# Squares without a ring slot, a weight ring in reverse, and retention products with two heads in turn, in a transformer layer on one core

## The chip, the cores and the metric

The kernel runs on one core of a Trainium2 chip. The core has five engines with instruction streams of their own: TensorE (PE; its weight loads are shown as PEld), VectorE (DVE), ScalarE (ACT), GpSimd (POOL) and SyncE (SP), which issues most of the DMAs. They meet only in semaphores. The metric is the device time of one execution in microseconds; of several timed runs the median counts.

## The reference

One layer over 1024 tokens of width 1024, in float32: a norm, one input projection, a gated causal convolution, an eight-head retention, a mix of the two, a mixture of 32 experts (two for each token) and a gated addition of a second input p.

```python
h = rmsnorm(x, g_mix)
u, c_g, b_g, q, k, v, sg, m_c, m_r = split(h @ w_in)
y_conv = (b_g * causal_dwconv(c_g * u, conv_w)) @ w_out_conv
q, k = rope(q), rope(k) * RET_DK ** -0.5          # 8 heads of 64
o = retention(q, k, v)                             # v: 8 heads of 128
y_ret = (silu(sg) * rmsnorm(o, g_ret)) @ w_out_ret
x = x + (sigmoid(m_c) * y_conv + sigmoid(m_r) * y_ret) @ w_o
x = x + hier_moe(rmsnorm(x, g_moe), ...)
ple = rmsnorm(p @ w_ple_proj, g_ple_post)
x = x + sigmoid(rmsnorm(x, g_ple_in) @ w_ple_gate) * ple
return rmsnorm(x, g_final)

def retention(q, k, v):      # chunks of 128 tokens; state: 64 x 128 for each head
    for each chunk:
        scores = (qb @ kb.T) * decay_mask
        inner  = scores @ vb
        cross  = (qb @ state) * q_decay
        state  = state * chunk_decay + (kb * k_decay).T @ vb
        out    = inner + cross
```

## The kernel before

The program runs in stages, whose times in the profiled execution are: the norm of x, its transpose and the projection to q, k, v, in two halves of 512 tokens (0 to 208 us); the gate sg with one retention chunk in each of eight steps (208 to 441); the convolution and the other gates (441 to 744); the mix and its projection (744 to 1020); the router and the projection of p (1020 to 1062); 32 experts (1062 to 1640); the last gate and norm (from 1646).

**Products.** Most matmuls work on a split: `split` (lines 186 to 190) has ScalarE write the high part of a tile (L188) and VectorE the rest (L189), and `mm3` (L193, L194, L195) multiplies high by high, high by low and low by high. The third needs the low part of its left operand. The retention's own products (scores L335, outputs L349 and L353, kv L369) are plain float32, and the trace shows each of them as two instructions.

**Order.** The program is written as one sequence; a scheduler sets the order on each engine by its own estimates, within what `tc.issue_after` binds. An engine then works through its order strictly, so an instruction that waits holds all behind it. Tiles come from pools: a pool's tag has a number of slots, and the first write to a tile waits until the tile that last held the slot has been read, by a DMA too. The tag `w2k` has ten slots of 2 KB a partition (`NW = 10`) and serves most scratch tiles.

**Squares.** `sumsq` (L218 to L222) takes the sum of squares of a block of 128 tokens on ScalarE; its elementwise output, which nothing reads, goes to a `w2k` slot (`xssj`). In `norm_T` (L224) each of the four blocks of a half is squared, scaled on VectorE by its rstd (`xrs`, `xi`, L235), transposed on TensorE (`xtq`, `xtp`, L240) and split into `ha` and `hb`, from which the projection `qa` reads. In `ple` (L781) the square `pj` (L805) of each half block takes a slot too, and so does the product `po` (L806, L807), which a DMA writes to the buffer `pled` in DRAM (L808): sixteen such transfers in all.

**Retention.** `retention(n, ck)` gives four steps that are put between the seven products of a gate pair: `turned` (transposes of q and k), `scores`, `outputs`, `close`. Tile `qt[r, a_]` holds in rows 0 to 63 head 2·a_ and in rows 64 to 127 head 2·a_+1, so a product of one head uses half the rows of TensorE. `scores` does the four even heads into bank `tr`, then the four odd ones into bank `S`. `outputs` fills one bank with heads 0 to 3 and one with heads 4 to 7: scores times v, and the state product of two heads at once, whose state tile is zero where the heads do not belong together. The next chunk's `turn` transposes the result and writes it to `od`.

**Experts.** The weights come as halves h = 0, 1, 2, ... of 1 MB into `raw` tiles (L746). `prep` (L921) splits each into one of three buffers `hls[h % RING]`: high part on ScalarE (L928), low part on VectorE (L930). `expert_x` (L942) transposes the gathered tokens (`xp`, L949) and splits them (`xh`, `xl`). These pools are opened where those of the stages before end, so `xl` and the buffers of the ring wait, at their first write, for the last use of what lay at their addresses.

Of the kernel before, what the change touches and what calls it, by code (L numbers as in the profile page):

```python
# [12 lines left out]
BF = mybir.dt.bfloat16  # L13
I32 = mybir.dt.int32
AF = mybir.ActivationFunctionType
OP = mybir.AluOpType
# [14 lines left out]
NW = 10  # L31
# [44 lines left out]
def tile_kernel(ctx, tc, cst, x, p, g_mix, w_in, conv_w, g_ret, w_out_conv, w_out_ret, w_o, g_moe,  # L76
# [140 lines left out]

    def sumsq(src, name, pool=wk):  # L218
        s = pool.tile([128, 8], F32, name=name, tag="sm", bufs=4)
        j = pool.tile([128, 1024], BF, name=name + "j", tag="w2k", bufs=NW)  # L220
        A.activation(j, src, AF.Square, accum_out=s[:, 0:1])
        return s[:, 0:1]  # L222

    def norm_T(hf, xi, gx):  # L224
# [67 lines left out]
    def bank(name, tag):  # L292
        return ps.tile([128, 4, 128], F32, name=name, tag=tag, bufs=1)

    def turn(n):
        t0 = n * 128
        for b in range(2):
            pt = bank("otp", ("o", "kv")[b])
            for j in range(4):
                pe = T.transpose(pt[:, j], osb[b][:, j], ident).ins  # L300
            ot = w2k("ot").rearrange("p (a b) -> p a b", a=4)
            for j in range(4):
                A.activation(ot[:, j], pt[:, j], AF.Copy, scale=gret[:, 4 * b + j:4 * b + j + 1])
            Y.dma_start(out=od[b * 512:(b + 1) * 512, t0:t0 + 128].rearrange("(a p) t -> p a t", p=128), in_=ot)
        return pe


    def retention(n, ck):
        first, last = n == 0, n == 7
        Y.dma_start(out=ck, in_=qd[n * 128:(n + 1) * 128])  # L310
        q, k, v = ck[:, 0:512], ck[:, 512:1024], ck[:, 1024:2048]
        qt, kt = (w2k(n_).rearrange("p (a b) -> p a b", a=4) for n_ in ("qt", "kt"))
        sm, rss, kvs = [], [], []

        def turned(pe):
            for src, dst_, tag in ((q, qt, "tr"), (k, kt, "S")):
                pt = bank("qkp", tag)
                for a_ in range(4):
                    pe = T.transpose(pt[:, a_], src[:, a_ * 128:(a_ + 1) * 128], ident).ins
                if src is q:  # L320
                    V.tensor_tensor(dst_, pt, qdT, op=OP.mult)
                else:
                    A.activation(dst_, pt, AF.Copy)
            if not first:
                with tc.issue_after(pe):
                    pe = turn(n - 1)
            return pe

        def scores(pe):
            for par in range(2):  # L330
                sp = bank("sp", ("tr", "S")[par])
                r = slice(par * 64, par * 64 + 64)
                with tc.issue_after(pe):
                    for a_ in range(4):
                        pe = T.matmul(sp[:, a_], kt[r, a_], qt[r, a_], start=True, stop=True).ins  # L335
                sb = w2k("sb").rearrange("p (a b) -> p a b", a=4)
                V.tensor_tensor(sb, sp, caus[:, None, :].to_broadcast([128, 4, 128]), op=OP.mult)
                sm.append(sb)
            return pe

        def outputs(pe):
            for b in range(2):
                op = bank("op", ("o", "tr")[b])
                m_ = 0
                with tc.issue_after(pe):
                    for a_ in (2 * b, 2 * b + 1):
                        for par in range(2):
                            h = 2 * a_ + par
                            pe = T.matmul(op[:, h - 4 * b], sm[par][:, a_], v[:, h * 128:(h + 1) * 128],  # L349
                                          start=m_ == 0, stop=first, skip_group_check=True).ins  # L350
                            m_ += 1
                        if not first:
                            pe = T.matmul(op[:, (a_ % 2) * 2:(a_ % 2) * 2 + 2], qt[:, a_],  # L353
                                          state[:, a_].rearrange("p (u v) -> p u v", u=2), start=False, stop=True,
                                          skip_group_check=True).ins
                A.activation(osb[b], op, AF.Copy)
                sq = w2k("osq").rearrange("p (a b) -> p a b", a=4)
                A.activation(sq, op, AF.Square)
                ss = wk.tile([128, 8], F32, name="oss", tag="sm", bufs=4)
                V.tensor_reduce(ss[:, 0:4], sq, axis=AX.X, op=OP.add)  # L360
                rss.append(rstd(ss[:, 0:4], DV, "ors"))
            if last:
                return pe
            kvs.append(bank("kv", "kv"))
            with tc.issue_after(pe):
                for a_ in range(4):
                    for par in range(2):
                        h = 2 * a_ + par
                        pe = T.matmul(kvs[0][par * 64:par * 64 + 64, a_], k[:, h * 64:h * 64 + 64],  # L369
                                      v[:, h * 128:(h + 1) * 128], start=True, stop=True, skip_group_check=True).ins  # L370
            return pe

        def close():
            for b in range(2):
                V.tensor_tensor(osb[b], osb[b], rss[b][:, :, None].to_broadcast([128, 4, 128]), op=OP.mult)
            for par in range(0 if last else 2):
                r = slice(par * 64, par * 64 + 64)
                sv = state[r, :, par * 128:par * 128 + 128]
                V.tensor_tensor(sv, sv, kvs[0][r], op=OP.add)
                V.tensor_tensor(sv, sv, Gd[r, :, None].to_broadcast([64, 4, 128]), op=OP.mult)  # L380

        return [turned, scores, outputs, close]


# [397 lines left out]
    def ple(wpl, pin):  # L782
# [12 lines left out]
        for t in range(8):  # L795
            pp = pps[t]
            for b in range(2):
                cc = slice(b * 512, (b + 1) * 512)
                a = acc("pa")
                for k in range(2):  # L800
                    r0 = k * 1024 + b * 512
                    mm3(a, pp[:, 0, k], pp[:, 1, k], wpl[:, r0:r0 + 512], wpl[:, 2048 + r0:2560 + r0],
                        k == 0, k == 1)
                j = w2k("pj", BF)[:, 0:512]
                A.activation(j, a, AF.Square, accum_out=ss[:, t, b:b + 1])  # L805
                o = w2k("po")  # L806
                V.tensor_tensor(o, a, gp[b], op=OP.mult)  # L807
                Y.dma_start(out=pled[t * 128:(t + 1) * 128, cc], in_=o)  # L808
                if b == 0 and t < 6:
                    pps.append(turned(t + 2))  # L810
# [103 lines left out]


    hls = [t.rearrange("p (s n) -> p s n", s=2) for t in (first_hl, mt("ha"), mt("hb"))]
    hls[1:] = hls[:0:-1]
    done = [0]

    def prep(n):  # L920
# [346 lines left out]
```

## Time and profile before

| | |
|---|---|
| timed runs, us | 1774.49, 1774.91, 1778.44; median 1774.91 |
| profiled execution, us | 1771.04, of which span 1769.2 |
| TensorE busy, us | 1708.2 (97%), 8063 matmul instructions |
| VectorE, ScalarE, GpSimd busy, us | 1265.4, 903.2, 157.2 |
| mean granted clock of TensorE | 0.99 of full speed |
| DMA | 397.63 MB, 225 GB/s over the span |

Busy time is the time in which an engine had an instruction at work; matmuls overlap, so that the start of one to the start of the next is the time that one costs in a row. Where TensorE has no gap in a stage, time that its instructions give up is time off the span. The granted clock is given as a share of 2.4 GHz; 0.5 is 1.2 GHz.

### The profile page before, as it was taken

How to read it: one execution, taken by the hardware profiler on the slowest of the kernel's cores; microseconds unless marked ns; L12 is line 12 of the kernel's file. 1: busy time of each engine (PE TensorE's matmuls, PEld its weight loads, DVE VectorE, ACT ScalarE, POOL GpSimd, SP SyncE). 2: the span in 40 equal slices, each digit the busy share in tenths (PEclk: the TensorE clock that was granted, in tenths of full speed). 3: DMA queues.
4: the chain of work that ended last, by engine and by line, in shares of the span. 5: the costliest groups of instructions: out<-in, count | busy, mean ns of one | idle time of the engine just before them, and what ended most of it. 6: DMA issues, size and time to landing. Idle time of an engine off the chain costs nothing.

```text
span 1769.2 us, 22046 instructions
## 1 busy us (share of the span) xinstructions
PE 1708.2 (97%) x8063; PEld 1325.2 (75%) x8063; DVE 1265.4 (72%) x1748; ACT 903.2 (51%) x1326; POOL 157.2 (9%) x157
## 2 busy tenths in 40 slices
PE   6999999999999999999999989999999999999697
PEld 5878788888888787788888866666666666666586
DVE  5559575666766775746455378999999988888674
ACT  4343344444222223524322257788888877778542
POOL 1000000000000000000000012222212121100010
PEclk9999999999999999999999999999999999999899
DMA  7534434444113226657556799999999999996561
GB/s 231 151 104 138 157 120 146 130 135 137 60 60 95 72 86 185 203 180 249 180 166 208 268 297 365 350 374 389 366 381 362 382 362 349 373 395 259 211 255 58
DMA packets 166401, 397.63 MB, mean 225 GB/s; under 512 B 14764, under 2 KB 85492, under 8 KB 140692
## 3 DMA queue, kind: packets, MB, share of 16 engines
q1 hardware_dynamic: 156788, 378.19, 61.3%
q0 software_dynamic: 9504, 18.02, 3.4%
q8 instruction: 64, 1.05, 0.2%
q14 instruction: 45, 0.37, 0.1%
HBM read 344.77 MB, written 57.68 MB: 227 GB/s over the span
## 4 chain that ended last, share of the span: by engine, by line
PE 74%; issue 13%; DMA 6%; DVE 4%; ACT 1%; POOL 0%; SPq 0%; POOLq 0%; DVEq 0%; ACTq 0%
PE y L193 4%; PE y L195 4%; PE y L194 4%; PE qa L193 3%; PE qa L195 3%; PE qa L194 3%; PE g L193 3%; PE g L194 3%; PE g L195 3%; PE u L194 3%; PE u L193 3%; PE u L195 3%; DMA both<-in_w_in_dram 3%; PE sd L193 2%; PE sc L193 2%
## 5 line engine op out<-in xcount | busy, mean ns | idle before, releaser
L930 DVE TENSOR_TENSOR hc<-raw,hc 128x1024 fp32r<-128x1024 f32 x128 | 154.3, 1223 | 20.4 <-ACT hc L928 19.2
L930 DVE TENSOR_TENSOR hb<-raw,hb 128x1024 fp32r<-128x1024 f32 x128 | 153.9, 1219 | 15.5 <-ACT hb L928 14.2
L930 DVE TENSOR_TENSOR ha<-raw,ha 128x1024 fp32r<-128x1024 f32 x128 | 154.1, 1222 | 13.7 <-ACT ha L928 11.7
L188 ACT ACTIVATE pc<-both 128x512 fp32r<-128x512 f32 x120 | 75.1, 629 | 157.4 <-PE sc L195 86.0
L928 ACT ACTIVATE ha<-raw 128x1024 fp32r<-128x1024 f32 x128 | 132.7, 1058 | 26.6 <-PE y L195 15.3
L928 ACT ACTIVATE hb<-raw 128x1024 fp32r<-128x1024 f32 x128 | 132.8, 1057 | 21.2 <-PE u L195 11.6
L928 ACT ACTIVATE hc<-raw 128x1024 fp32r<-128x1024 f32 x128 | 132.5, 1056 | 14.5 <-PE y L195 5.7
L189 DVE TENSOR_TENSOR pc<-both,pc 128x512 fp32r<-128x512 f32 x120 | 82.1, 686 | 27.0 <-ACT pc L188 26.6
L193 PE MATMUL y<-ph,wys 128*128 128x512 f32 x248 | 97.1, 392 | 1.9 <-ACT wys L188 1.9
L195 PE MATMUL y<-ph,wys 128*128 128x512 f32 x248 | 96.5, 390 | 0.0
L194 PE MATMUL y<-pl,wys 128*128 128x512 f32 x248 | 96.5, 389 | 0.0
L188 ACT ACTIVATE wys<-wyr 128x1024 fp32r<-128x1024 f32 x31 | 32.8, 1061 | 99.7 <-PE y L195 79.3
L193 PE MATMUL sd<-sh,pc 128*128 128x512 f32 x192 | 76.2, 397 | 3.8 <-DVE u L454 3.8
L195 PE MATMUL sd<-sh,pc 128*128 128x512 f32 x192 | 74.9, 390 | 0.0
L194 PE MATMUL sd<-sl,pc 128*128 128x512 f32 x192 | 74.8, 390 | 0.0
L189 DVE TENSOR_TENSOR wqs<-wqr,wqs 128x1024 fp32r<-128x1024 f32 x32 | 39.1, 1222 | 49.1 <-ACT wqs L188 49.1
L188 ACT ACTIVATE wqs<-wqr 128x1024 fp32r<-128x1024 f32 x32 | 33.9, 1059 | 70.2 <-PE qa L195 63.8
L769 POOL DMA_INDIRECT xgb<-h2d,ii x32 | 36.2, 1130 | 294.6 <-DVE hd L966 198.5
L188 ACT ACTIVATE pc<-bt 128x512 fp32r<-128x512 f32 x48 | 30.3, 630 | 62.7 <-PE sa L195 25.3
L558 DVE TENSOR_TENSOR msg<-y,msg 128x512 f32<-128x512 f32 x32 | 22.1, 690 | 53.7 <-PE y L195 53.7
L448 ACT ACTIVATE u<-sa 128x512 f32<-128x512 f32 x24 | 14.3, 597 | 84.1 <-PE sa L195 44.8
L193 PEld LDWEIGHTS y<-ph,wys 128*128 128x128 f32 x248 | 46.6, 188 | 12.1 <-ACT wys L188 2.8
(400 smaller groups left out, 4837.4 us busy)
## 6 DMA issues: line engine op xcount, KB each, us to landing
raw<-in_w_exp_gate_dram SPq DMA_DIRECT2D x64, 1024.0 KB, 19.7
raw<-in_w_exp_up_dram SPq DMA_DIRECT2D x64, 1024.0 KB, 17.6
raw<-in_w_exp_down_dram SPq DMA_DIRECT2D x63, 1024.0 KB, 18.8
both<-in_w_in_dram SPq DMA_DIRECT2D x24, 1024.0 KB, 5.7
wqr<-in_w_in_dram SPq DMA_DIRECT2D x32, 512.0 KB, 3.8
qd<-r SPq DMA_DIRECT2D x32, 256.0 KB, 2.4
both<-qd SPq DMA_DIRECT2D x8, 1024.0 KB, 4.8
wyr<-in_w_out_conv_dram SPq DMA_DIRECT2D x16, 512.0 KB, 3.8
```

Of the source, the lines that this page charges most:

```text
L188: a = A.activation(hi, src, AF.Copy)
L189: V.tensor_tensor(lo, src, hi, op=OP.subtract)
L193: T.matmul(o, lh, rh, start=start, stop=False, skip_group_check=skip)
L194: T.matmul(o, lh, rl, start=False, stop=False, skip_group_check=skip)
L195: return T.matmul(o, ll, rh, start=False, stop=stop, skip_group_check=skip).ins
L448: A.activation(u2, a, AF.Copy)
L558: V.tensor_tensor(sg, y, sg, op=OP.mult)
L769: g = P.indirect_dma_start(out=xgs[e % 3], out_offset=None, in_=h2d, in_offset=bass.IndirectOffsetOnAxis(ap=ii[:, 0, e:e + 1], axis=0), bo ...
L928: A.activation(hl[:, 0, q:q + 1024], raw[:, q:q + 1024], AF.Copy)
L930: V.tensor_tensor(hl[:, 1, q:q + 1024], raw[:, q:q + 1024], hl[:, 0, q:q + 1024], op=OP.subtract)
```

## The change

It has three parts.

1. The squares write their elementwise output to memory that is there anyway and is not read at that time: those of `sumsq` to the first 2 KB of `shared`, which later holds the retention state, those of `ple` to columns of `pint`. They take no slot of `w2k` any more.
2. In `scores` the two heads of a pair alternate. In `outputs` the state products come first, one for each head (64 rows, 128 columns, where it was 128 rows and 256 columns for two heads), the two heads of a pair in turn and each into a bank of its own; then come the products of scores and v. A bank now holds the heads of one parity, and `turn` and the rows of `od` follow.
3. The ring of weight buffers is `hb, ha, hc` instead of `hc, hb, ha`.

```diff
     def sumsq(src, name, pool=wk):
         s = pool.tile([128, 8], F32, name=name, tag="sm", bufs=4)
-        j = pool.tile([128, 1024], BF, name=name + "j", tag="w2k", bufs=NW)
-        A.activation(j, src, AF.Square, accum_out=s[:, 0:1])
+        A.activation(shared[:, 0:512].bitcast(BF), src, AF.Square, accum_out=s[:, 0:1])
...
-                A.activation(ot[:, j], pt[:, j], AF.Copy, scale=gret[:, 4 * b + j:4 * b + j + 1])
-            Y.dma_start(out=od[b * 512:(b + 1) * 512, t0:t0 + 128].rearrange("(a p) t -> p a t", p=128), in_=ot)
+                A.activation(ot[:, j], pt[:, j], AF.Copy, scale=gret[:, 2 * j + b:2 * j + b + 1])
+            Y.dma_start(out=od.rearrange("(a u p) t -> u p a t", u=2, p=128)[b, :, :, t0:t0 + 128], in_=ot)
...
         def scores(pe):
+            sp = [bank("sp", ("tr", "S")[par]) for par in range(2)]
+            for a_ in range(4):
+                for par in range(2):
+                    r = slice(par * 64, par * 64 + 64)
+                    with tc.issue_after(pe):
+                        pe = T.matmul(sp[par][:, a_], kt[r, a_], qt[r, a_], start=True, stop=True).ins
             for par in range(2):
-                sp = bank("sp", ("tr", "S")[par])
-                r = slice(par * 64, par * 64 + 64)
-                with tc.issue_after(pe):
-                    for a_ in range(4):
-                        pe = T.matmul(sp[:, a_], kt[r, a_], qt[r, a_], start=True, stop=True).ins
                 sb = w2k("sb").rearrange("p (a b) -> p a b", a=4)
...
         def outputs(pe):
-            for b in range(2):
-                op = bank("op", ("o", "tr")[b])
-                m_ = 0
-                with tc.issue_after(pe):
-                    for a_ in (2 * b, 2 * b + 1):
-                        for par in range(2):
-                            h = 2 * a_ + par
-                            pe = T.matmul(op[:, h - 4 * b], sm[par][:, a_], v[:, h * 128:(h + 1) * 128],
-                                          start=m_ == 0, stop=first, skip_group_check=True).ins
-                            m_ += 1
-                        if not first:
-                            pe = T.matmul(op[:, (a_ % 2) * 2:(a_ % 2) * 2 + 2], qt[:, a_],
-                                          state[:, a_].rearrange("p (u v) -> p u v", u=2), start=False, stop=True,
-                                          skip_group_check=True).ins
+
+            ops = [bank("op", ("o", "tr")[b]) for b in range(2)]
+            for a_ in range(4) if not first else ():
+                for b in range(2):
+                    r = slice(b * 64, b * 64 + 64)
+                    with tc.issue_after(pe):
+                        pe = T.matmul(ops[b][:, a_], qt[r, a_], state[r, a_, b * 128:b * 128 + 128],
+                                      start=a_ == 0, stop=False, skip_group_check=True).ins
+            for b, op in enumerate(ops):
+                with tc.issue_after(pe):
+                    for a_ in range(4):
+                        h = 2 * a_ + b
+                        pe = T.matmul(op[:, a_], sm[b][:, a_], v[:, h * 128:(h + 1) * 128],
+                                      start=first and a_ == 0, stop=True, skip_group_check=True).ins
...
-                j = w2k("pj", BF)[:, 0:512]
-                A.activation(j, a, AF.Square, accum_out=ss[:, t, b:b + 1])
+                A.activation(pint[:, 3808:4064].bitcast(BF), a, AF.Square, accum_out=ss[:, t, b:b + 1])
...
     hls = [t.rearrange("p (s n) -> p s n", s=2) for t in (first_hl, mt("ha"), mt("hb"))]
-    hls[1:] = hls[:0:-1]
+    hls.reverse()
```

**TensorE, second retention chunk.** The names `sp` are the scores' two banks, `op` the outputs' two, `qt` and `kt` the transposed q and k, `sb` the masked scores, `shared` the state and `both` the chunk of q, k and v. Before:

```order
L195 MATMUL sd_1783<-sh_876,pc_1833 128x512
L335 MATMUL sp_1848<-qt_1773,kt_1774 128x128 x4
L335 MATMUL sp_1855<-qt_1773,kt_1774 128x128 x4
L193 MATMUL sa_1780<-ha_111,pc_1862 128x512
...
L195 MATMUL sa_1780<-ha_111,pc_1862 128x512
L349 MATMUL op_1882<-both_1568,sb_1853 128x128
L349 MATMUL op_1882<-both_1568,sb_1860 128x128
L353 MATMUL op_1882<-shared_81,qt_1773 128x256
...
L369 MATMUL kv_1912<-both_1568 64x128 x8
```

In the new program, at the same place:

```order
L195 MATMUL sd_1775<-sh_868,pc_1825 128x512
L334 MATMUL sp_1840<-qt_1765,kt_1766 128x128
L334 MATMUL sp_1841<-qt_1765,kt_1766 128x128
L334 MATMUL sp_1840<-qt_1765,kt_1766 128x128
L334 MATMUL sp_1841<-qt_1765,kt_1766 128x128
...
L334 MATMUL sp_1841<-qt_1765,kt_1766 128x128
L193 MATMUL sa_1772<-ha_111,pc_1854 128x512
...
L195 MATMUL sa_1772<-ha_111,pc_1854 128x512
L348 MATMUL op_1874<-shared_81,qt_1765 128x128
L348 MATMUL op_1875<-shared_81,qt_1765 128x128
...
L354 MATMUL op_1874<-both_1560,sb_1850 128x128 x4
L354 MATMUL op_1875<-both_1560,sb_1852 128x128 x4
L369 MATMUL kv_1908<-both_1560 64x128 x8
```

The scores change bank with every matmul; the state products stand together ahead of the products with v, as eight of 128 columns in two banks instead of four of 256.

**ScalarE, end of the projection's first half.** `qa` are its sums, `r0` their evacuations, `xi` the second half's tokens, `xss` a sum of squares, `ha` and `hb` the parts of the split. Before:

```order
L272 ACTIVATE r0_769<-qa_649 128x512
L272 ACTIVATE r0_772<-qa_650 128x512
L272 ACTIVATE r0_775<-qa_651 128x512
L272 ACTIVATE r0_778<-qa_652 128x512
L221 ACTIVATE xssj_789,xss_788<-xi_781 128x1024
L188 ACTIVATE wqs_966<-wqr_964 128x1024
L221 ACTIVATE xssj_811,xss_810<-xi_781 128x1024
L188 ACTIVATE ha_786<-xtq_795 128x4x128
L188 ACTIVATE hb_787<-xtp_803 128x4x128
```

In the new program:

```order
L188 ACTIVATE wqs_880<-wqr_878 128x1024
L188 ACTIVATE wqs_909<-wqr_907 128x1024
L271 ACTIVATE r0_765<-qa_645 128x512
L271 ACTIVATE r0_768<-qa_646 128x512
L271 ACTIVATE r0_771<-qa_647 128x512
L271 ACTIVATE r0_774<-qa_648 128x512
L188 ACTIVATE ha_782<-xtq_790 128x4x128
L188 ACTIVATE hb_783<-xtp_798 128x4x128
L220 ACTIVATE shared_81,xss_826<-xi_777 128x1024
L188 ACTIVATE ha_782<-xtq_811 128x4x128
```

The squares of the second half's first two blocks have left this place (they are now the 15th and 16th instruction of ScalarE's order, ahead of the first half's last copies), and the split of the first block follows the evacuations directly.

**VectorE, way into the experts, with what each instruction waits for.** `po` are the last products of `ple`, `prs` its rstd, `xl` the low part of the first expert's tokens; DMAHW3 and the like are the eight lanes in which SyncE's transfers are counted. Before:

```order
L807 TENSOR_TENSOR po<-pa,pin 128x512 [waits DVE_49,Activation_49]
L807 TENSOR_TENSOR po<-pa,pin 128x512 [waits Activation_49]
L811 TENSOR_TENSOR prs<-pss 128x8
L812 TENSOR_SCALAR prs<-prs 128x8 [waits DVE_49]
L930 TENSOR_TENSOR hc<-raw,hc 128x1024 [waits Activation_49] x2
L189 TENSOR_TENSOR xl<-xp,xh 128x352 [waits DMAHW4_49,DMAHW5_49,DMAHW0_49,Activation_49]
L189 TENSOR_TENSOR xl<-xp,xh 128x352 [waits Activation_49]
```

In the new program:

```order
L806 TENSOR_TENSOR po<-pa,pin 128x512 [waits DMAHW1_49,Activation_49]
L806 TENSOR_TENSOR po<-pa,pin 128x512 [waits DMAHW2_49,Activation_49]
L806 TENSOR_TENSOR po<-pa,pin 128x512 [waits Activation_49]
L810 TENSOR_TENSOR prs<-pss 128x8
L811 TENSOR_SCALAR prs<-prs 128x8 [waits DVE_49]
L189 TENSOR_TENSOR xl<-xp,xh 128x352 [waits DMAHW3_49,DMAHW0_49,Activation_49]
L189 TENSOR_TENSOR xl<-xp,xh 128x352 [waits Activation_49]
L929 TENSOR_TENSOR hb<-raw,hb 128x1024 [waits Activation_49]
```

`xl` waited for three transfers of `pled`, the last of them the thirteenth of sixteen; now the last that it waits for is the fifteenth. The split of `hc` no longer stands ahead of it.

## Rows read from the trace of the kernel before

**Rows 1.** The page, busy time of each engine: us, share of the span, instructions.

```profile
PE 1708.2 (97%) x8063; PEld 1325.2 (75%) x8063; DVE 1265.4 (72%) x1748; ACT 903.2 (51%) x1326; POOL 157.2 (9%) x157
```

**Rows 2.** Windows by stage: length, busy time of each engine, clock, DMA share, GB/s.

```profile
208.00:441.00 233.00, 232.67 (x1286) 193.66 (x1285) 153.40 (x251) 101.38 (x212) 16.43 (x16) 0.99 0.42 132
...
1020.00:1062.00 42.00, 32.76 (x203) 26.46 (x201) 31.00 (x87) 22.96 (x57) 7.16 (x5) 0.96 0.99 314
1062.00:1640.00 578.00, 575.75 (x2674) 395.02 (x2674) 513.65 (x523) 464.31 (x567) 107.88 (x92) 1.00 0.98 360
```

**Rows 3.** Windows, TensorE: scores, outputs and kv of the second chunk.

```profile
242.32:243.96 1.64, 1.64 (x18) 1.00 0.86 202
246.82:250.43 3.61, 3.61 (x25) 1.00 0.03 10
250.43:251.45 1.02, 1.02 (x17) 1.00 0.00 0
```

**Rows 4.** Scores, line 335: count, ns min/median/max, first and last start.

```profile
L335 PE MATMUL sp<-qt,kt x128: 272/272/373, 216.6 to 408.5; 64*128 64x128 f32 x128
```

**Rows 5.** Timeline, TensorE, second chunk: start, us, engine line op, tiles, shapes, count.

```profile
242.00 0.39 PE L195 MATMUL sd<-sh,pc 128*128 128x512 f32 x1
242.32 1.71 PE L335 MATMUL sp<-qt,kt 64*128 64x128 f32 x16
243.96 0.50 PE L193 MATMUL sa<-ha,pc 128*128 128x512 f32 x1
244.29 0.39 PE L194 MATMUL sa<-ha,pc 128*128 128x512 f32 x1
...
246.82 0.61 PE L349 MATMUL op<-both,sb 128*128 128x128 f32 x4
247.27 0.60 PE L353 MATMUL op<-shared,qt 128*128 128x256 f32 x2
247.70 0.61 PE L349 MATMUL op<-both,sb 128*128 128x128 f32 x4
```

**Rows 6.** Timeline and one window (columns as in rows 2), second norm; brackets: idle before.

```profile
109.23 1.05 ACT L221 ACTIVATE xssj<-xi 128x1024 bf16<-128x1024 f32 x1
...
111.29 1.41 DVE L235 SCALAR_TENSOR_TENSOR xi<-xi,xrs,gx 128x512 f32<-128x512 f32 x2 [0.73 <-POOL xrs L215]
...
112.14 0.63 PE L240 MATMUL xtq<-cs,xi 128*128 128x128 f32 x4 [3.44 <-issue]
...
112.20:116.70 4.50, 4.42 (x15) 3.07 (x16) 3.77 (x7) 2.39 (x6) 0.55 (x1) 0.62 0.37 92
```

**Rows 7.** Timeline, ScalarE and VectorE, end of the first norm.

```profile
24.19 1.06 ACT L188 ACTIVATE wqs<-wqr 128x1024 fp32r<-128x1024 f32 x1 [2.05 <-DMA wqr<-in_w_in_dram]
...
26.43 0.68 DVE L189 TENSOR_TENSOR ha<-xtq,ha 128x512 fp32r<-128x512 f32 x1
```

**Rows 8.** Timeline and one window (columns as in rows 2), way into the experts.

```profile
1054.19 1.02 PE L949 MATMUL xp<-cs,xgb 88*128 88x88 f32 x8
1057.31 2.79 SPq L808 DMA_DIRECT2D pled<-po  x2
1058.35 0.60 ACT L805 ACTIVATE pj<-pa 128x512 bf16<-128x512 f32 x1 [4.59 <-DMA pled<-po]
...
1059.79 2.00 ACT L928 ACTIVATE hc<-raw 128x1024 fp32r<-128x1024 f32 x2 [0.76 <-DVE po L807]
...
1062.20 0.73 PE L193 MATMUL g<-hc,xh 128*88 128x512 f32 x1 [6.99 <-ACT xh L188]
...
1063.73 0.73 PE L195 MATMUL g<-hc,xl 128*88 128x512 f32 x1
...
1064.72 0.43 POOL L952 COPY rs<-xgb 88x1 f32<-88x1 f32 x3 [2.92 <-DMA pled<-po]
...
1062.20:1066.00 3.80, 3.80 (x9) 2.10 (x10) 1.91 (x3) 0.55 (x2) 0.76 (x4) 0.56 0.99 407
```

More of the change, by code (lines that the diff above doesn't have):

```diff
@@ L329, in scores @@
         def scores(pe):
-            for par in range(2):
-                sp = bank("sp", ("tr", "S")[par])
-                r = slice(par * 64, par * 64 + 64)
-                with tc.issue_after(pe):
-                    for a_ in range(4):
-                        pe = T.matmul(sp[:, a_], kt[r, a_], qt[r, a_], start=True, stop=True).ins
+            sp = [bank("sp", ("tr", "S")[par]) for par in range(2)]
[4 more added lines that the diff above has]
+                        pe = T.matmul(sp[par][:, a_], kt[r, a_], qt[r, a_], start=True, stop=True).ins
+            for par in range(2):
                 sb = w2k("sb").rearrange("p (a b) -> p a b", a=4)
-                V.tensor_tensor(sb, sp, caus[:, None, :].to_broadcast([128, 4, 128]), op=OP.mult)
+                V.tensor_tensor(sb, sp[par], caus[:, None, :].to_broadcast([128, 4, 128]), op=OP.mult)
                 sm.append(sb)
```

## The prediction

> **What bounds the kernel now.** I read the page's busy line first, then the windows by stage, then the timeline of the places that the change touches. TensorE is busy 1708.2 of 1769.2 us (97%) [rows 1]. The windows by stage show why only TensorE time counts where the change works: in the retention stage TensorE is busy 232.67 of 233 us while VectorE has 153 and ScalarE 101, so an instruction that leaves TensorE there shortens the span by as much as it took, and work moved on the other two is covered [rows 2]. The experts are the same for TensorE (575.75 of 578) with the DMA at 0.98. Between them, 1020 to 1062, TensorE has 9.2 us without work. Two idle stretches lie on the places that the change touches: 3.44 us at 112.14, and 6.99 us at 1062.20 [rows 6, 8]. After each the granted clock is low: means of 0.62 and 0.56 over the next stretch [rows 6, 8], the lower of the two levels (1.2 GHz) for most of it.
>
> The sum is made in the profiled execution: 1771.04 us, of which 1769.2 are span. The three timed runs have a median of 1774.91, 3.9 above it; I take the differences over to that median.
>
> **Scores (8 chunks).** Eight matmuls of 64 rows, x16 as the trace counts instructions; the first four pairs use rows 0 to 63, the next rows 64 to 127. In the second chunk they hold TensorE 1.64 us [rows 3]; all eight chunks are alike (x128, a median of 272 ns from start to end, pipelined [rows 4]). Part of this is already shared: one such instruction behind another takes 0.11 us (x4 from 246.82 to 247.27 [rows 5]), and the last one begins at 242.32 + 1.71 − 0.27 = 243.76, 0.20 ahead of the next matmul, 0.09 more than a step; sixteen steps and this would be 1.85. The nearest row for strict turns is the kv product: also 16 instructions, in turn on two halves of the array's columns, in 1.02 us [rows 3]. After the change the scores take turns on two halves of the rows and write two banks. I take 1.02: 0.62 off, times 8 = **5.0 us**. Bounds: if row halves only follow one another, the present overlap is lost too, 1.85 against 1.64, +1.7 in all; if they run as closely as eight steps of 0.109 without a change of shape, 0.87, −6.2.
>
> **Outputs (7 of 8 chunks; the first has no state).** Before, outputs take 3.61 us [rows 3]: 16 instructions of 0.109 for sb·v, and 8 of 256 columns at 0.22 for the state (x2 in 0.43, 247.27 to 247.70 [rows 5]), so 1.75 + 1.73 + 0.1 for the entry into kv. After, the state part is 16 instructions of half the rows and half the columns, in turn: 8 steps of 0.109 = 0.87. It adds a change of shape where there was none. The rows price one: a 512-column matmul takes 0.23 (eleven from 244.29 to 246.82); the entry into the scores takes 0.32 (242.00 to 242.32), leaving them 0.09 more than a step, and the second matmul after them starts 0.33 behind the first (243.96 to 244.29) [rows 5]: 0.09 + 0.09 + 0.10, about 0.29 together. So 1.75 + 0.87 + 0.1 + 0.29 = 3.0: 0.57 off, times 7 = **4.0 us**. Bounds: +0.3 a chunk, +2.1, if the halves follow one another (16 of 0.109 for the same 1.73); −0.86 a chunk, −6.0, if the change of shape is free.
>
> The first state product of the second bank needs that bank free of the scores, 1.3 us (sb·v of four and state) earlier than before; a block of twelve sa matmuls of 2.9 us lies between [rows 5], and VectorE is a third idle there [rows 2], so I add no wait. Its price, should the masking come late, is 0.2 to 0.5 a chunk. Both parts together: −9.0; I take −8.7, leaving 0.3 for such ends. The reordered gains and output rows have the same sizes and cost nothing.
>
> On the change of shape the Trainium skill speaks against this edit: TensorEngine Tiling (Array Packing), Key Properties, says that "Changing tiling mode (not just tile) drains the TensorE", while different tiles run in parallel. The rows agree with a small price (0.29); if a drain cost a whole pipeline of the 0.5 us that one matmul lasts at entry and at exit, the sum of this part would be −8.7 + 7 × 0.7 = −3.8.
>
> **Squares' scrap, second norm.** Before, the square of the second half's first block stands in ScalarE's order behind the last evacuations: 109.23, then xrs and the scaling 111.29, the transpose 112.14; TensorE idles 3.44 us, and the clock then averages 0.62 from 112.20 to 116.70, which costs about 4.5 × 0.38 = 1.7 [rows 6]. After, that square and the next one stand among the first 16 rows of ScalarE, and two blocks are scaled long before. The transposes follow the last qa directly. What is late next: the split of the first block. Its high part needs ScalarE, which the evacuations leave free at 109.23 [rows 6], so the first qa starts at about 109.9, and the low part (0.68 on VectorE, as at 26.43 [rows 7]) feeds the third matmul at about 110.6; the second block's copies stand behind one more square of 1.05. I count 1 us of such gaps, where 5.1 stood; −4.1, less 0.6 for later ones (the fourth block's scaling stands behind a fill of the shared tile, which moves here from the start) = −3.5. On the other side, at the start, ScalarE gets two squares (2.4 us) into an idle of 2.05 in front of 24.19, and VectorE gets two scalings of 0.70 in front of the low split at 26.43 [rows 7], which moves by two scalings and takes up the 0.8 or so that TensorE has in hand for it (eight matmuls of 0.23 behind the transposes): +0.6. Sum **−2.9**; bounds 0 (the chain of copies takes all) and −5.1.
>
> **Scrap and ring at the way into the experts.** Before, the last square waits for its ring slot, that is for a transfer of pled: ScalarE idle 4.59 until 1058.35; then po, then hc, whose buffer opens when po is done (1059.79); then xh, and TensorE, whose transposes were done by 1055.2, resumes at 1062.20 and has its first low product, which waits for xl, at 1063.73 [rows 8]. After, squares take no slot, and the weight ring begins with hb and ha, which are split early; that whole chain ends near 1057. What is late next is xl: by the order its first write now waits for the fifteenth pled transfer (DMAHW3), where it waited for the thirteenth. In the trace the last two leave at 1057.31, because their queue holds them behind weights, and the gather's weights rs, which wait for the fifteenth, start at 1064.72 after 2.92 us of waiting [rows 8]. The DMA is busy 0.99 there, so an earlier po does not make it land earlier. xl then begins at about 1064.6, and its first product follows 0.6 later (the split of a 128x352 half, by 0.68 for 128x512 [rows 7]): 1065.2 instead of 1063.73. By then two matmuls are done; the clock is down again after 8 us of waiting, and takes as long to return as it did before (1062.20 to about 1065.5), so at 1068.6 ten matmuls are done, where before there were 7 + 3.1/0.23 = 20. Ten of 0.23: **+2.3**. Behind xl on VectorE stand the low parts of hb and hc; hc is due at about 1071.5, when TensorE comes to it. Bounds: −7 (no wait in xl, first matmuls at 1057) and +4.
>
> **Sum.** −8.7 − 2.9 + 2.3 = −9.3: 1761.7 in the profiled execution, **1765.5** by the median. The experts' DMA (0.98) is met 2 us later in step and gives nothing back. Everything else changes only by which ring slot falls where; ±1.
>
> **Rivals.** (a) xl's wait does not bind: pled lands early, since the po behind it are done sooner and no square holds a slot. Then the 7 us come back besides: −8.7 − 2.9 − 7 = −18.6, 1756. Against it: the transfer is held by its queue and by weights, not by po. (b) Row halves do not run side by side: +1.7 + 2.1 with the other terms at −2.9 + 2.3 gives +3.2, 1778; within no change. Against it: sixteen score instructions in 1.64 need some overlap between the halves already. (c) Slower: the new wait at xl, whose place is the 15th pled. It decides when another pair of 1 MB weights goes ahead of it: 2.1 MB at the 407 GB/s of that stretch [rows 8] is 5 us more, so the term is 2.3 + 5 = 7.3; and with the row halves worth nothing (between the forecast and (b)) the sum is −2.9 + 7.3 = +4.4, 1779. For it: the DMA is full, and its order has moved.
>
> **Chances.** Forecast 0.62; (a) 0.16; (b) 0.11; (c) 0.07; a rest of 0.04 shared. About 0.2% (3.5 us) is what a measurement can tell from no change: faster 0.80, same 0.12, slower 0.08. The likeliest case's own range is 1760 to 1770 (terms at half their bounds); the range to hold 8 of 10 takes in (a) and most of the way to (b): 1756 to 1774.
>
> **What would show it.** Windows over a chunk: scores 1.0 instead of 1.64, outputs 3.0 instead of 3.61; the gap at 112 gone or below 1.5 us, and no low clock behind it. At the experts: a wait of xl for pled, two matmuls near 1057 and then 7 to 9 us without TensorE work, the third matmul some 11 us behind the transposes where it came 9.5 behind (1054.19 to 1063.73 [rows 8]). I am wrong if the scores stay at 1.6 or if TensorE resumes for good near 1057.

## The result, and the profile after

The changed kernel takes 1762.45 us in the median of its first timed runs, against 1775.68 for the kernel before: a ratio of 0.9925 (95% interval 0.9907 to 0.9942), some 13 us faster. The forecast was 1765.5, inside a range of 1756 to 1774. The direction and the places were right; the gain is 4 us above the forecast of 9.3, which lies just below its interval (10 to 17 us).

The page after, its busy line, to be set beside [rows 1]:

```profile
PE 1700.6 (97%) x8119; PEld 1317.7 (75%) x8119; DVE 1264.3 (72%) x1748; ACT 901.0 (51%) x1326; POOL 159.9 (9%) x157
```

TensorE has 7.6 us less work; VectorE and ScalarE have theirs as before. The span is 1759.5.

**The second retention chunk.** Windows over its scores, its outputs and its kv, columns as in [rows 3]:

```profile
236.53:237.63 1.10, 1.10 (x18) 1.00 0.85 217
240.57:243.65 3.08, 3.08 (x34) 1.00 0.14 42
243.65:244.67 1.02, 1.02 (x17) 1.00 0.00 0
```

and the timeline of TensorE there, columns as in [rows 5]:

```profile
236.53 1.16 PE L334 MATMUL sp<-qt,kt 64*128 64x128 f32 x16
...
240.57 1.16 PE L348 MATMUL op<-shared,qt 64*128 64x128 f32 x16
241.67 2.05 PE L354 MATMUL op<-both,sb 128*128 128x128 f32 x16
```

The scores take 1.10 where they took 1.64, the outputs 3.08 where they took 3.61. The block of state products has the same 1.16 as the scores, which have the same shape.

**The second norm.** Timeline, and windows over this place and over the first products of the gates (columns as in [rows 2]):

```profile
109.17 0.60 PE L239 MATMUL xtq<-cs,xi 128*128 128x128 f32 x4
...
109.86 0.59 ACT L188 ACTIVATE ha<-xtq 128x512 fp32r<-128x512 f32 x1
...
110.51 0.50 PE L193 MATMUL qa<-wqs,ha 128*128 128x512 f32 x1 [0.30 <-ACT ha L188]
...
108.80:123.00 14.20, 13.54 (x73) 10.58 (x72) 10.25 (x17) 8.02 (x14) 1.10 (x2) 1.00 0.40 136
204.10:211.36 7.26, 7.25 (x33) 5.27 (x34) 5.79 (x10) 3.68 (x7) 0.00 (x0) 1.00 0.11 40
```

The transposes follow the last qa without a wait, TensorE is idle for 0.66 us in all of the stretch, and the clock stays up. The last row is a surprise. The same stretch of the kernel before, from the first sb product to the first scores, behind the product that opens it (first line before, second after; brackets: idle before):

```profile
207.76 0.50 PE L193 MATMUL sb<-sh,pc 128*128 128x512 f32 x1 [1.53 <-ACT pc L188]
204.11 0.50 PE L193 MATMUL sb<-sh,pc 128*128 128x512 f32 x1 [1.53 <-ACT pc L188]
...
207.70:216.58 8.88, 8.82 (x33) 6.24 (x33) 5.79 (x10) 3.73 (x8) 0.00 (x0) 0.81 0.09 32
```

Both kernels come to it behind a gap of 1.53 us; before, the clock fell behind the gap (mean 0.81 of the stretch), after, it did not (1.00), and that is 1.6 us more.

**The way into the experts.** Timeline, after, to be set beside [rows 8]:

```profile
1043.92 1.12 PE L948 MATMUL xp<-cs,xgb 88*128 88x88 f32 x8 [0.57 <-DMA xgb<-h2d,ii]
...
1052.39 0.96 DVE L189 TENSOR_TENSOR xl<-xp,xh 128x352 fp32r<-128x352 f32 x2 [7.26 <-DMA pled<-po]
1052.97 0.73 PE L195 MATMUL g<-hb,xl 128*88 128x512 f32 x1 [7.12 <-DVE xl L189]
```

The wait that was forecast is there: xl stands for 7.26 us behind a pled transfer and TensorE for 7.12 behind xl. It ends 9.1 us behind the transposes, where the first low product came 9.5 behind them before.

### The profile page after: what moved, and what is told of

It reads as the page before. It is cut to its first block, busy times and chain, and to the rows that moved or that the text cites. A ratio compares the mean times of both kernels' runs of the same rounds, so it can differ in the third digit from the quotient of the medians.

```text
span 1759.5 us, 22143 instructions
## 1 busy us (share of the span) xinstructions
PE 1700.6 (97%) x8119; PEld 1317.7 (75%) x8119; DVE 1264.3 (72%) x1748; ACT 901.0 (51%) x1326; POOL 159.9 (9%) x157
## 4 chain that ended last, share of the span: by engine, by line
PE 79%; DMA 7%; DVE 6%; issue 6%; ACT 2%; POOL 0%; SPq 0%; POOLq 0%; DVEq 0%; ACTq 0%
PE y L193 6%; PE y L195 6%; PE y L194 6%; PE g L195 3%; PE g L194 3%; PE g L193 3%; PE u L194 3%; PE u L193 3%; PE u L195 3%; DMA both<-in_w_in_dram 3%; PE qa L194 2%; PE qa L195 2%; PE qa L193 2%; PE sd L193 2%; PE sc L193 2%
## 5 line engine op out<-in xcount | busy, mean ns | idle before, releaser
L927 ACT ACTIVATE ha<-raw 128x1024 fp32r<-128x1024 f32 x128 | 132.6, 1056 | 20.3 <-PE u L195 11.3
```

Of the source, the lines that this page charges most:

```text
L927: A.activation(hl[:, 0, q:q + 1024], raw[:, q:q + 1024], AF.Copy)
```

## The experiments

Stages are compared by the starts of TensorE's first products: the first `sb` of the gates, the first and the eighth chunk's scores, the first `y` and `oa` of the mix, the first `pa`, the first expert's transposes `xp` and the second's; the first row ends where the last qa of the projection's first half has made way (its start and a step of 0.23). "Before again" and the like are second profiles of the same program. Lengths in us, one profiled execution each:

| from, to | before | before again | changed | changed again | xl moved | xl moved again |
|---|---|---|---|---|---|---|
| start, last qa of the first half | 108.5 | 109.8 | 109.2 | 110.5 | 109.5 | 110.1 |
| to sb | 99.2 | 99.8 | 94.9 | 95.0 | 94.9 | 94.9 |
| to the first scores | 8.8 | 8.7 | 7.2 | 7.2 | 7.2 | 7.2 |
| to the eighth chunk's scores | 190.5 | 190.5 | 183.9 | 184.2 | 183.9 | 184.1 |
| to y | 330.1 | 330.8 | 328.8 | 330.3 | 330.2 | 330.0 |
| to oa | 89.6 | 89.6 | 91.1 | 89.7 | 89.6 | 91.0 |
| to pa | 201.7 | 202.5 | 203.0 | 203.1 | 202.4 | 202.0 |
| to the first xp | 25.7 | 27.3 | 25.7 | 30.7 | 26.8 | 27.5 |
| to the second xp | 20.8 | 20.3 | 21.4 | 21.9 | 14.0 | 14.0 |
| to the end of the span | 694 | 695 | 694 | 695 | 694 | 694 |

**Each kernel once more.** The changed kernel and, later, the one before.

> The changed kernel once more. Theory: the profiled executions differ by 9.7 us of span (1769.2 and 1759.5), and that is the change; the 13 us between the first medians hold a few us of chance, so here 8 to 11 us off, ratio 0.9940 to 0.9955. Rival: the timed executions of the kernel before lose something that its profile does not show, and 13 us (0.9925) come again.

Measured: 1763.66 against 1775.12, 0.9925 (0.9912 to 0.9939). The rival held: 13 us again. The profile, however, came out at 1767.9 of span, 8 us above the first; it is the slowest of the five executions of this measurement (1769.6; the others 1761.0 to 1764.1). Its rows at the way into the experts:

```profile
1050.82 1.44 PE L948 MATMUL xp<-cs,xgb 88*128 88x88 f32 x8 [5.61 <-DMA xgb<-h2d,ii]
...
1058.73 0.96 DVE L189 TENSOR_TENSOR xl<-xp,xh 128x352 fp32r<-128x352 f32 x2 [11.73 <-DMA pled<-po]
1059.31 0.73 PE L195 MATMUL g<-hb,xl 128*88 128x512 f32 x1 [5.93 <-DVE xl L189]
```

In this execution the first expert's gather landed 5 us later behind its issue than in the first profile, with the same program.

> The kernel before, for a second profile. Theory: it is the first profile (1771.0, 4 us below the timed median of 1775.1) that is a fortunate execution; here the span is 2 to 5 us longer, in places outside the change's parts: the start, a fall of the clock behind the gap at the mix, the way into the experts. Rival: profiled executions are shorter than timed ones as such, and this one has 1769 of span again.

Measured: a span of 1774.1. The theory held: the first profile of the kernel before was a fortunate one. The table's two columns of one kernel differ by up to 5 us in a single row, and the rows that differ by more than 1 us are the start, the eighth scores to y, y to oa (a clock that falls or not behind a gap) and pa to xp (with the DMA busy nearly throughout). One pair of profiles gives the size of a term only where the rows of the same kernel agree.

**The retention alone.** The parts of `scores`, `outputs` and `turn` in the kernel before, nothing else.

> The kernel before with the retention's part alone (scores and state products in turn, the two banks by parity). Theory: scores 1.09 instead of 1.64 in 8 chunks, outputs 3.08 instead of 3.61 in 7, 7.5 to 8 us off; the gap of 3.4 us at the second norm and the 7 us ahead of the experts stay. Rival: the retention is worth less than its windows (the freed time comes back as waits for masks or evacuations): 3 us off or less.

Measured: 1772.8 against 1775.12, 0.9980 (0.9970 to 0.9989): 3.5 us faster (2.0 to 5.3), half of what was expected. The windows held (183.9 from the first to the eighth scores, as in the changed kernel). But the way into the experts was longer, 23.8 us from xp to the second xp instead of 20.8. Its timeline:

```profile
1060.31 0.73 PE L193 MATMUL g<-hc,xh 128*88 128x512 f32 x1 [6.46 <-ACT xh L188]
...
1063.41 0.95 DVE L189 TENSOR_TENSOR xl<-xp,xh 128x352 fp32r<-128x352 f32 x2 [2.06 <-DMA pled<-po]
1063.99 0.73 PE L195 MATMUL g<-hc,xl 128*88 128x512 f32 x1 [2.11 <-DVE xl L189]
```

The ring of scratch slots falls otherwise in this program, and xl lies where a late pled transfer reads. Whether that is the whole of the missing 4 us is tried by leaving the retention out where this wait is short (below).

**The squares of the norm alone.** The first hunk of the change in the kernel before.

> The kernel before with the scrap of sumsq alone moved out of the ring. Theory: the gap at the second norm goes (3.44 us and the low clock behind it), the first sb product of the gates comes at 204 instead of 207.8; 3 to 5 us off. Rival: the gain of that place in the changed kernel belongs to another ring position of the whole program, and here it is 0 to 1 us.

Measured: 1769.3, 0.9964 (0.9950 to 0.9978): 6.4 us (3.9 to 8.9). Last qa to sb takes 94.8 instead of 99.2, sb to the first scores 7.2 instead of 8.8, with the clock at 1.00 (the window of this run):

```profile
205.62:212.88 7.26, 7.22 (x34) 5.26 (x34) 5.79 (x10) 3.71 (x7) 0.00 (x0) 1.00 0.11 40
```

The start is 0.7 us longer on average over nine profiles with the scrap moved (110.1; 109.1 to 111.0) than over four without (109.4; 108.5 to 110.3). That has the size of the +0.6 forecast for the two squares put there, but the two groups overlap, so it is not shown. Every one of the four profiles with the stall at the second norm shows the low clock behind the gap at sb (lengths 8.7 to 8.8), and none of the nine without it (7.2 to 7.3); the gap itself is 1.53 in twelve of them and 1.59 in one of the nine. What the one has to do with the other, 95 us earlier, was not tried.

**The scrap of p's squares and the ring alone.**

> The kernel before with the scrap of ple's squares and the reversed weight ring alone. In this order xl waits for the fourteenth pled transfer, which goes ahead of the pair of weights that the fifteenth stands behind. Theory: what this part is worth is set by the transfer on which xl falls; here it lands 1 to 3 us earlier than the fifteenth would, and the second transposes of the experts come 1 to 4 us sooner after the end of the products of p than in the kernel before (21 us); the stall at the second norm stays. Time 1 to 5 us below the kernel before. Rival: ring and scrap take the 7 us of idle time away by themselves (7 to 9 us below), or cost (above).

Measured: 1775.1 against 1776.18, 0.9996 (0.9985 to 1.0007), at the lower edge of what was expected or less. The profile has the mechanism: xl waits 3.07 us for its transfer instead of 7.26 in the changed kernel, and xp to the second xp is 18.1.

```profile
1061.26 0.96 DVE L189 TENSOR_TENSOR xl<-xp,xh 128x352 fp32r<-128x352 f32 x2 [3.07 <-DMA pled<-po]
1061.84 0.73 PE L195 MATMUL g<-hb,xl 128*88 128x512 f32 x1 [3.32 <-DVE xl L189]
```

Of those 2.7 us hardly any is in the timed runs (0.7, −1.2 to 2.7). The profiled execution is the fastest of the ten, and with the ring reversed the stretch ahead, oa to pa, is longer (below), so the profile alone does not give this part's worth.

**xl at another address.** Two tiles of later use are taken from the pool ahead of xl, so that its buffer lies on a slot whose last pled transfer is an early one.

```diff
         xh = mw.tile([128, 8, CAP], F32R, name="xh", tag="xh", bufs=2)
+        if e == 0:
+            early.append(mw.tile([CAP, 512], F32, name="hd", tag="hd", bufs=2))
+            early.append(mw.tile([128, 4, CAP], F32R, name="th"))
         xl = mw.tile([128, 8, CAP], F32R, name="xl", tag="xl", bufs=2)
...
-        hd = mw.tile([CAP, 512], F32, name="hd", tag="hd", bufs=2)
+        hd = early.pop(0) if e == 0 else mw.tile([CAP, 512], F32, name="hd", tag="hd", bufs=2)
...
-        th = mw.tile([128, 4, CAP], F32R, name="th")
+        th = early.pop() if early else mw.tile([128, 4, CAP], F32R, name="th")
```

> The changed kernel, with the buffer of the first expert's xl at an address whose last user is an early pled transfer (two tiles are taken from the pool ahead of it). Theory: the 7.1 us that TensorE waits for xl at the way into the experts are that transfer alone; the low product comes within 3 us of the transposes instead of 9, the clock does not fall, 6 to 8 us below the changed kernel. Rival 1: hc, whose split waits in ScalarE's order behind hb, ends last next, and 1 to 3 us remain of it: 4 to 6 us below. Rival 2: the experts then catch up with their weights (DMA 0.98) and give it back: 0 to 2 us below.

Measured: 1753.51, 0.9869 (0.9854 to 0.9884), 10 us below the changed kernel. The timeline:

```profile
1044.52 1.12 PE L953 MATMUL xp<-cs,xgb 88*128 88x88 f32 x8 [1.62 <-DMA xgb<-h2d,ii]
1045.24 0.91 ACT L188 ACTIVATE xh<-xp 128x352 fp32r<-128x352 f32 x2 [1.55 <-PE xp L953]
1045.73 0.97 DVE L189 TENSOR_TENSOR xl<-xp,xh 128x352 fp32r<-128x352 f32 x2 [1.04 <-ACT xh L188]
...
1046.31 0.46 PE L195 MATMUL g<-hb,xl 128*88 128x512 f32 x1
```

xl starts as soon as xh is there, the low product comes 1.8 us behind the transposes, and xp to the second xp takes 14.0 instead of 21.4: 7.4 us, within the theory's 6 to 8 (the timed 10 is above them), and nothing of it is given back by the experts (694 us from the second xp to the end, as without this edit). One thing in the expectation was wrong: the clock does fall there; of the 4 us from 1048 on the mean is 0.74, part at the lower level and part at full speed:

```profile
1048.00:1052.00 4.00, 4.00 (x15) 2.57 (x14) 2.83 (x3) 3.92 (x5) 1.75 (x2) 0.74 1.04 427
```

Repeated:

> The version with xl's buffer moved once more, beside the run without the retention's part. Theory: again 9 to 11 us below the changed kernel's 1763 (1752 to 1755), since neither xl nor hc waits. Rival: the first run was fortunate, 1757 or more.

Measured: 1756.6 against 1776.85, 0.9885 (0.9869 to 0.9900): a little above what was expected, 20 us below the kernel before and, by the ratios, 7 below the changed kernel; the profile again has 14.0. In both measurements this version is faster than both kernels (0.9869 and 0.9885, where the changed kernel has 0.9925).

**The order of the weight ring.** The old order (`hls[1:] = hls[:0:-1]`), in the changed kernel and in the one with xl moved.

> The changed kernel with the weight ring in its old order (hc first). Theory: while xl waits for the fifteenth pled transfer, hc and the xh behind it are done in its shadow, so the first low product comes when it did: within 1.5 us of the changed kernel. Rival: the ring's order is what the way into the experts gains, and 4 to 7 us are lost.

Measured: 1766.21, 0.9954 (0.9939 to 0.9968), against 0.9925 for the changed kernel: 5 us worse by the ratios, 2 to 9 with their intervals. In the profile, though, it is as forecast, with a span of 1759.2: hc and xh are done in the shadow of xl, whose product comes at the same time of the execution as in the changed kernel (1052.5 and 1053.0). Counted from the first pa it comes 1.6 us later; the stretch oa to pa is 1.4 shorter.

```profile
1045.92 0.73 PE L193 MATMUL g<-hc,xh 128*88 128x512 f32 x1 [3.09 <-ACT xh L188]
...
1052.46 0.73 PE L195 MATMUL g<-hc,xl 128*88 128x512 f32 x1 [4.95 <-DVE xl L189]
```

The profiled execution is the fastest of the five of this kernel (1761.0; the others 1765.4 to 1767.5), so the profile may not show what the others lost. Theory and rival each have half of it; open.

> The version with xl's buffer moved, with the weight ring in its old order. Theory: with xl early, hc ends last (its buffer opens with the last po, and xh stands behind its split on ScalarE): 1.5 to 3 us above the version with the reversed ring, still 6 to 8 below the changed kernel. Rival: the order is worth nothing here either (within 1 us).

Measured: 1760.35, 0.9919 (0.9901 to 0.9937), against 0.9869 and 0.9885 in the two measurements with the reversed ring: about 9 or 6 us, more than the theory's 1.5 to 3. The profile shows the mechanism:

```profile
1046.51 2.00 ACT L927 ACTIVATE hc<-raw 128x1024 fp32r<-128x1024 f32 x2 [0.76 <-DVE po L806]
...
1048.42 0.80 ACT L188 ACTIVATE xh<-xp 128x352 fp32r<-128x352 f32 x2
```

hc waits for the last po, and xh behind it on ScalarE starts 3.6 us after xp, where it was 0.7 with the ring reversed. The second xp comes 17.1 behind the first instead of 14.0. That is 3 of the 6 to 9; the profiled execution was again the fastest of its kernel, and the rest stays open.

**Turns or size.** The state products as four of one half and then four of the other.

```diff
-            for a_ in range(4) if not first else ():
-                for b in range(2):
+            for b in range(2) if not first else ():
+                for a_ in range(4):
```

> The changed kernel with the state products as four of one half of the rows and then four of the other, instead of in turn. Theory: it is the turns that make the halves run side by side; the block takes 1.6 us as the old scores did, instead of 1.1, so the outputs lose their whole gain of 0.53, times 7 = 3.7 us above the changed kernel. Rival: products of half the size are enough, and the time stays (within 1 us).

Measured: 1768.24, 0.9964 (0.9950 to 0.9978), 4.6 us above the changed kernel by the medians (7 by the ratios, of which half is within their intervals). The timeline:

```profile
242.02 1.71 PE L348 MATMUL op<-shared,qt 64*128 64x128 f32 x16
243.66 2.05 PE L354 MATMUL op<-both,sb 128*128 128x128 f32 x16
```

1.71 in blocks, 1.16 in turn, for the same instructions into the same two banks: the outputs' whole gain is in the turns. (In turn the bank changes with every matmul too; no run has the halves in turn in one bank.) The first to the eighth scores took 187.2 instead of 183.9, which is 0.55 for each of the six chunks between.

**Without the retention, where xl is early.**

> The version with xl's buffer moved, without the retention's part (scores and outputs as in the kernel before); xl again waits for an early pled transfer only (its buffer lies behind three tiles instead of two, since the ring falls otherwise). Open is why the retention alone was worth 3.5 us in the timed runs where its windows save 7.6. Theory: it is worth its windows, and that run lost 3 to 4 us again at the way into the experts, where xl fell on a later transfer; where the way into the experts is short in both, leaving it out costs 7 to 8 us. Rival: the retention's gain is partly given back wherever it stands, and leaving it out costs 3 to 4 us.

Measured: 1766.49, 0.9939 (0.9925 to 0.9952), beside 1756.6 on the same chip: 9.9 us worse (by the ratios 6 to 13). From the first to the eighth scores it takes 190.5 again. xl still waited a little here:

```profile
1056.85 0.96 DVE L189 TENSOR_TENSOR xl<-xp,xh 128x352 fp32r<-128x352 f32 x2 [2.96 <-DMA pled<-po]
1057.43 0.73 PE L195 MATMUL g<-hb,xl 128*88 128x512 f32 x1 [0.91 <-DVE xl L189]
```

and xp to the second xp is 15.8, 1.9 above. What remains is 8 us for the retention (4 to 11 with the interval), its windows' worth. The rival (3 to 4 us, part of it given back wherever it stands) lies at the lower edge of that or below: the retention alone looked small mostly because that program lost 3 us at xl.

## Why the prediction was right, and where its terms were off

**Scores and outputs: right, a little too large.** Forecast −8.7. By the windows the scores give 0.54 for each of 8 chunks and the outputs 0.53 for each of 7, 8.0 together. From start to start it is less, 6.6 between the first and the eighth scores, since entering the state block costs 0.32 from the last sa product instead of 0.23; with the last chunk some 7.6. The nearest row, kv, was 0.08 too good: its second pair of turns starts 0.16 behind the first and the others 0.109 apart, where the scores have 0.21 and 0.112, so that the block takes 1.10 instead of 1.02. The prediction also misread when the second bank is needed: its first product stood 1.75 us behind the first bank's before (248.58 against 246.82), not 1.3; no wait came of it. The page TensorEngine Tiling (Array Packing) of the Trainium skill, Key Properties, which has a change of mode drain the array, is borne out as a small price only: the state block costs 1.10 for eight steps of 0.11, the 0.2 behind its last start included. The same section of the Trainium skill has different tiles run in parallel; that shows here for products in turn (1.16 against 1.71 us in blocks).

**The second norm: right, its size too small.** Forecast −2.9, with −5.1 as the bound; measured −4.5 to sb, −1.5 behind it and perhaps +0.7 at the start, −5.3 (timed alone −6.4, with 3.9 to 8.9 as the interval). Two terms failed. I counted 1.6 us of new gaps; there are 0.66 in 14 us (0.30 for a high part and 0.34 for a low part), and the other transposes and products stand without a wait. And the prediction has no term for the low clock behind the gap at sb; it went with the stall.

**The way into the experts: the mechanism right, its size and its chance missed.** The wait at xl came, for the transfer named. I had it end 11 us behind the transposes; it ended 9.1 behind them in the first profile and 8.5 in the second. The step that failed was that the queue holds this transfer behind weights, so that it lands when it did before, however early po is. Before, counted from the first pa, the fifteenth po was done at 26.0 and its transfer left at 28.8; the queue had waited for a pair of gate weights to land. In the second profile of the changed kernel it did so again (first line before, second changed again: total, times, longest):

```profile
SPq L808 <- DMA raw<-in_w_exp_gate_dram: 3.2, 1, 3.2
SPq L807 <- DMA raw<-in_w_exp_gate_dram: 4.3, 1, 4.3
```

In the first profile of the changed kernel that wait does not occur: the transfer left at 25.3, directly behind its po (25.2), and xl began at 34.2, 2 us sooner than the transfer landed before (36.2). In the second it left at 29.0, and xl began at 38.6. In the second profile of the kernel before it was not held either (po 27.6, left 27.8). So an earlier po does bring the transfer forward in an execution in which the gate weights have landed by then. The prediction took the last two transfers to leave together at 1057.31; that row merges two, and the sixteenth left at 1059.8, at the end of its own po.

From xp to the second xp the term was +0.6 and +1.1, for a forecast of +2.3. From the first pa on, which takes in the wait for the gather, it was +0.6 in the first profile (46.5 to 47.1) and +6.1 in the second (52.6), the slowest execution of its kernel. What no term held is the order that the scheduler makes around the reversed ring. All seven profiles with it have a wait of 0.99 us at the router that none of the other six has, and oa to pa takes 202.8 us in their mean, against 201.8. The gather of the first expert is issued 16.5 to 16.8 us after the first pa in the seven, and 14.7 or 16.2 in the six:

```profile
1012.54 1.13 PE L616 MATMUL lp<-xgb,h2T 128*128 128x96 f32 x8 [0.99 <-DVE h2T L613]
...
1034.78 1.18 POOL L769 DMA_INDIRECT xgb<-h2d,ii  x1 [17.94 <-DMA raw<-in_w_exp_down_dram]
```

The transposes wait for the gather in all seven, 0.57 us in the first profile of the changed kernel and 5.61 in the second, and in none of the six. Rival (a), 1756 if the wait at xl does not bind, was priced about rightly: with xl moved, the time is 1753.5 and 1756.6, though the wait went with the address there and not, as the rival had it, with an earlier po.

**The sum.** Profile to profile it came out at −9.7, the forecast's −9.3, but partly by luck: −7.6, −5.3 and +0.6 make −12.3; against it stand +1.5 at y to oa, which the repeats put down to chance, and +1.2 from oa to pa, where the waits are 0.99 more at the router, 0.68 more among the first oa and 0.56 less ahead of the first pa. The timed 13 us (10 to 17 by the interval) allow these terms. The parts timed one by one (3.5, 6.4 and 0.7) add up to 10.6; with their intervals that does not contradict 13, and each falls on other slots at the way into the experts.

## What to carry to other kernels

Products of half the array's rows paid here when the two halves came in turn, each half into a bank of its own; the same instructions in two blocks gave the whole gain away. Where tiles of a new stage lie on the addresses of an old one, look up for each first write which transfer it waits for: an address decided 7 us here, about as much as the whole change of the retention, and an edit elsewhere can move it. A transfer that stands behind others in its queue can still leave sooner, so ask of each execution what its queue waited for. Compare a term between two profiles only after two profiles of one kernel have shown how far that stage moves by itself.

## What the hardware showed that was not expected

- The clock behind the gap of 1.53 to 1.59 us at sb fell in all four profiles of kernels with the stall at the second norm and in none of the nine without. Behind a gap of 1.7 to 2.0 some 7 us after the first y, which all have, it fell in five of the thirteen, without a pattern that these runs show (over the 4 us behind it the mean was 0.58 in the first profile of the changed kernel and 1.00 in that of the kernel before). Each fall costs about 1.5 us.
- With the DMA share at 1.0, the first expert's gather of the same program landed 9.1 us after its issue in one execution of the changed kernel (issued at 1034.78, TensorE released at 1043.92) and 14.2 in another (1036.64 to 1050.82).
